# A mixture-of-experts block: normalised rows in the gather, scale and bias at its eviction

## The chip, the cores and the metric

The kernel runs on one core of a Trainium2 chip. The metric is the device time of one execution in microseconds (us). Three runs of the kernel before took 1916.12, 1918.36 and 1924.67 us; the median is 1918.36 us.

## The reference

All data are float32. `x` is (1, 256, 1024): 256 tokens of 1024 values. The kernel computes two blocks in one launch. The change lies in the first one, between its mixer and its experts:

```python
h = layer_norm(x, ln_in_g, ln_in_b)
m = gated_mixer(h, ...)                                   # attention branches, gates, w_out
h = layer_norm(DEEPNORM_ALPHA * h + m, ln1_g, ln1_b)      # "LN1": (x - mean) * rsqrt(var + eps) * g + b
f = moe_ffn(h, ...)
h = layer_norm(DEEPNORM_ALPHA * h + f, ln2_g, ln2_b)

def moe_ffn(t, ...):                                      # 32 experts, top 4
    logits = t @ w_router + b_router
    top_val, top_idx = top_k(logits, 4)
    gate = softmax(top_val)
    # for each expert e, on the rows of t routed to it:
    hb = rows @ w_exp_in[e] + b_exp_in[e]                 # 1024 x 2048
    g, u = min(hb[:, :1024], 7), clip(hb[:, 1024:], -7, 7)
    y = (g * sigmoid(1.702 * g) * (u + 1)) @ w_exp_out[e] + b_exp_out[e]
    # and the gate-weighted sum of a token's four rows
```

The second block (conditioned norms, a recurrent mixer, an attention and two MLPs) follows and is not touched.

## The kernel before

Tokens lie in two tiles of 128 (t = 0, 1). The mixer ends with the product with `w_out` and `join`, which leaves the sum in `x_tm`. Then comes what is here called the routing (L747 to L825). For each t VectorE takes mean and variance, GpSimd the power -0.5 (`rsqrt_g`, L189), VectorE normalises in place (L784). TensorE transposes the normalised rows (L790), VectorE and ScalarE evict them to `h1T`, and eight matmuls with the router's weights `wr` give the logits (L800). `wr` already has the norm's scale in it, and `brt` the router's bias with the norm's bias. VectorE finds the four largest (MAX8, FIND_INDEX8, L803 to L805) and builds the mask `M` of 128 tokens by 32 experts (L806, L808). Four small matmuls turn the masks into each token's rank within its expert (L818 to L821). Beside this chain `h1`, the rows that the experts read, gets the norm's scale and bias: the product for t = 0 on VectorE (L798), the one for t = 1 and both additions on GpSimd (L811, L813). `bcs` holds scale and bias spread over all partitions.

Each expert has 64 slots. `gather` builds the selection masks `sel` (VectorE, L886: slot number equal to rank) and multiplies `h1` by them on TensorE (L895), in two halves of four 128-column groups; each half is evicted by one ScalarE copy (L897) into `xg`, the experts' rows with the features on the partitions. From expert 2 on one gather serves two experts, which makes it 128 wide. The weights come as tiles of 2 MB, six per expert, through three rings of SBUF buffers (3, 4 and 1 tiles), all issued on SyncE's queue.

`step(e)` is written out for each expert: `up_tile` 0 (L922, names pg and pu); in odd steps the gather for the next two experts, first half; the transposes of the expert before (aT); `up_tile` 1; the transposed scatter mask (sT); `down_tile` (py, L953) of the expert before and its copy ys; `up_tile` 2; the gather's second half; `combine`; `up_tile` 3; the SwiGLU on VectorE and ScalarE. `combine` multiplies ys by sT into four banks pc (L966), and VectorE adds each to the accumulator `facc` (L971), which has the memory of `bcs`. Before each expert's tiles its bias is put into the two accumulating banks by matmuls with a column of the identity (L771); `first_bias` does this for experts 0 and 1 during the routing. `facc_init` after step 0 sets `facc` to ALPHA times `h1` (L995). PSUM has two tags ("b" and "g") of four banks each, handed out in turn; gathers, transposes, py and pc share "b".

What is wrapped in `keep` or `pin` stands on its engine (TensorE, SyncE's queue) in the order of the code. The other instructions are placed by a scheduler, and `issue_after(x)` keeps them behind x. Each engine runs its own queue in order and waits on semaphores. Between steps 20 and 21 a loop serves experts with more than 64 rows; on these inputs it has no turn, but the engines meet at its barrier.

Of the kernel before, what the change touches and what calls it, by code (L numbers as in the profile page):

```python
# [72 lines left out]
def tile_kernel(  # L73
# [668 lines left out]
    wo = [wcols(w_out[0], 0, 1024, k0=4 * i, kc=4, pool=ring, pin=True) for i in range(2)]  # L742
    spread(ln1_g, ln1_b)
    o = [banks("wo") for _ in range(2)]

# [28 lines left out]
    def first_bias(e, i):  # L774
        expert_bias(first_acc[e][i], ident[:, 4 * e:4 * e + 4], i, keep)

    pl = bank("lg")
    h1T = [tmp("h1T") for _ in range(4)]
    mv = small("ln1mv", 4).rearrange("p (t k) -> p t k", t=2)
    rs = small("ln1r", 2)  # L780
    for t in range(2):
        stats(x_tm[:, t], t, mv, "ln1")
        rsqrt_g(rs[:, t:t + 1], mv[:, t, 1:2], 1e-5)
        normed = V.tensor_scalar(x_tm[:, t], x_tm[:, t], mv[:, t, 0:1], rs[:, t:t + 1], op0=ALU.subtract, op1=ALU.mult).ins  # L784
    first_bias(0, 0)
    for t in range(2):
        for hf in range(2):
            p = bank("h1T")
            for c in range(4):
                keep(T.transpose(p[:, c * 128:(c + 1) * 128], x_tm[:, t, (4 * hf + c) * 128:(4 * hf + c + 1) * 128],  # L790
                                 ident))
            if hf:
                S.copy(h1T[2 * t + 1], p)
            else:
                V.tensor_copy(h1T[2 * t], p)
        if t == 0:
            with tc.issue_after(normed):
                V.tensor_tensor(h1[:, 0], x_tm[:, 0], bcs[:, 0], op=ALU.mult)  # L798
        for k in range(8):
            keep(T.matmul(pl[:, 32 * t:32 * t + 32], h1T[2 * t + k // 4][:, (k % 4) * 128:(k % 4 + 1) * 128], wr[:, k, :], start=k == 0,  # L800
                          stop=k == 7, skip_group_check=True))
        V.tensor_tensor(lg[:, t], pl[:, 32 * t:32 * t + 32], brt, op=ALU.add)
        V.max(m8[:, t], lg[:, t])  # L803
        V.max_index(i8[:, t], m8[:, t], lg[:, t])
        V.tensor_copy(f8[:, t], i8[:, t])  # L805
        V.tensor_scalar(Mr[:, t], slot_i[:, 0:32], f8[:, t, 0:1], None, op0=ALU.is_equal)  # L806
        for j in range(1, 4):
            V.scalar_tensor_tensor(Mr[:, t], slot_i[:, 0:32], f8[:, t, j:j + 1], M[:, t],  # L808
                                   op0=ALU.is_equal, op1=ALU.add)
    with tc.issue_after(mark["G"]):  # L810
        G.tensor_tensor(h1[:, 1], x_tm[:, 1], bcs[:, 0], op=ALU.mult)  # L811
        for t in (1, 0):
            G.tensor_tensor(h1[:, t], h1[:, t], bcs[:, 1], op=ALU.add)  # L813

    first_bias(0, 1)
    first_bias(1, 0)
    pr = bank("rank")
# [5 lines left out]
    V.tensor_scalar(rr, rr, -1.0, None, op0=ALU.add)  # L823
    first_bias(1, 1)
    V.tensor_copy(cnt, pr[:, 64:96])  # L825
# [54 lines left out]
    def gather(rank_aps, pin=lambda i: i):  # L880
# [9 lines left out]
        def half(hf):  # L890
            p = bank("xg")
            for kc in range(4):
                i, r = divmod(4 * hf + kc, 2)
                for t in range(2):
                    pin(T.matmul(p[:, kc * 128:kc * 128 + w], h1[:, t, 256 * i + r:256 * (i + 1):2], sel[:, t, 0:w],  # L895
                                 start=t == 0, stop=t == 1))
            S.copy(xg[:, 4 * hf:4 * hf + 4, 0:w], p.rearrange("p (k s) -> p k s", k=4)[:, :, 0:w])  # L897

# [92 lines left out]
    def facc_init():  # L991
        next(ada0, None)
        with tc.issue_after(first_sel):
            for t in range(2):
                V.tensor_scalar(facc[:, t], h1[:, t], ALPHA, None, op0=ALU.mult)  # L995

# [691 lines left out]
```

## Time and profile before

| | |
|---|---|
| runs, median | 1918.36 us (1916.12 to 1924.67) |
| the profiled execution | 1921.77 us |
| its span, first to last instruction | 1920.0 us |
| mean granted TensorE clock | 0.972 |
| TensorE busy | 1833.3 us, 95% |
| VectorE, ScalarE, GpSimd busy | 799.4, 557.3, 91.1 us |
| DMA | 595.84 MB, mean 310 GB/s |

The span is one execution recorded on the chip. The busy shares are averages over stages with different limits, so the views below are read by stage. PEclk is the granted TensorE clock as a share of full speed, 1.00 for the upper level and 0.50 for the lower; a value between them is a mean over a stretch. DMA share is the mean busy share of the core's 16 DMA engines.

### The profile page before, as it was taken

The numbers are of one execution on the slowest core, as the hardware profiler recorded it, in microseconds if no ns is written. First come the engines' busy times: TensorE is split into PE (matmuls) and PEld (weight loads), VectorE is DVE, ScalarE is ACT, GpSimd is POOL, SyncE is SP. The second block draws the span as 40 slices with busy tenths as digits, with TensorE's granted clock in tenths as the row PEclk, the third lists the DMA queues.
The fourth block names the chain that finished last, engine by engine and source line by source line (L and its number), as shares of the span: only waits on it lengthen the run. The fifth ranks groups of instructions, "written<-read, shape, count | busy, mean of one in ns | idle before, by whom it ended". The sixth has DMA issues, their size and how long they took to land.

```text
span 1920.0 us, 23489 instructions
## 1 busy us (share of the span) xinstructions
PE 1833.3 (95%) x9861; PEld 1106.0 (58%) x9861; DVE 799.4 (42%) x1388; ACT 557.3 (29%) x869; POOL 91.1 (5%) x106
## 2 busy tenths in 40 slices
PE   7999989999999999985999999899999999999999
PEld 6867743333333333322333333688888965778997
DVE  6756741121211221220221122667754465665555
ACT  4645301110011110000101110554544454564443
POOL 3000100000000000000000000200100011000000
PEclk9989979998999999997999999999999999999999
DMA  8667868998999999998999999774666565434452
GB/s 291 243 219 264 346 252 330 428 420 360 425 427 428 427 428 427 428 427 336 427 428 427 428 427 416 268 254 148 250 252 249 213 239 179 153 131 154 176 196 89
DMA packets 100302, 595.84 MB, mean 310 GB/s; under 512 B 7533, under 2 KB 8002, under 8 KB 75362
## 3 DMA queue, kind: packets, MB, share of 16 engines
q1 hardware_dynamic: 85874, 540.68, 69.9%
q0 software_dynamic: 14288, 53.63, 8.0%
q8 instruction: 78, 1.28, 0.3%
q14 instruction: 30, 0.25, 0.0%
q10 hardware_dynamic: 32, 0.01, 0.0%
HBM read 593.24 MB, written 1.06 MB: 310 GB/s over the span
## 4 chain that ended last, share of the span: by engine, by line
PE 80%; DMA 8%; issue 5%; DVE 4%; POOL 1%; ACT 1%; SPq 0%; POOLq 0%; DVEq 0%; ACTq 0%
PE pg L922 11%; PE py L953 11%; PE pu L922 11%; PE xg L895 4%; DMA w<-in_w_exp_in_dram 4%; DMA wa<-in_ada_w_dram 3%; PE hid L271 3%; PE hid L270 3%; PE hid L269 3%; PE pc L966 3%; PE acc L254 3%; PE acc L255 3%; PE acc L256 3%; PE adp L628 2%; PE pu L771 2%
## 5 line engine op out<-in xcount | busy, mean ns | idle before, releaser
L199 DVE TENSOR_TENSOR wl<-w,wh 128x1024 fp32r<-128x1024 f32 x244 | 301.2, 1235 | 231.5 <-ACT wh L198 230.9
L971 DVE TENSOR_TENSOR bcs<-bcs,pc 128x512 f32<-128x512 f32 x124 | 76.9, 682 | 661.5 <-PE pc L966 661.5
L198 ACT CAST wh<-w 128x1024 fp32r<-128x1024 f32 x244 | 255.9, 1049 | 315.3 <-PE acc L256 85.2
L922 PE MATMUL pg<-w,xg 128*64 128x512 f32 x1016 | 262.0, 605 | 1.2 <-DMA w<-in_w_exp_in_dram 1.2
L922 PE MATMUL pu<-w,xg 128*64 128x512 f32 x1016 | 257.1, 595 | 0.0
L953 PE MATMUL py<-w,aTs 128*64 128x512 f32 x1024 | 226.8, 595 | 0.0
L922 PEld LDWEIGHTS pu<-w,xg 128*64 128x64 f32 x1016 | 73.6, 138 | 147.1 <-issue 147.1
L922 PEld LDWEIGHTS pg<-w,xg 128*64 128x64 f32 x1016 | 67.8, 138 | 139.0 <-issue 131.6
L953 PEld LDWEIGHTS py<-w,aTs 128*64 128x64 f32 x1024 | 70.7, 137 | 133.2 <-issue 132.7
L270 PE MATMUL hid<-xhl,wh 128*128 128x256 f32 x512 | 145.4, 284 | 0.0
L271 PE MATMUL hid<-xhl,wl 128*128 128x256 f32 x512 | 145.3, 284 | 0.0
L269 PE MATMUL hid<-xhl,wh 128*128 128x256 f32 x512 | 145.2, 284 | 0.0
L270 PEld LDWEIGHTS hid<-xhl,wh 128*128 128x128 f32 x512 | 98.5, 192 | 2.2 <-issue 1.7
L269 PEld LDWEIGHTS hid<-xhl,wh 128*128 128x128 f32 x512 | 98.5, 192 | 2.1 <-ACT xhl L1255 1.7
L271 PEld LDWEIGHTS hid<-xhl,wl 128*128 128x128 f32 x512 | 98.5, 192 | 0.8 <-issue 0.8
L897 ACT COPY xg<-xg 128x512 f32<-128x512 f32 (+1 forms) x34 | 19.0, 560 | 265.8 <-PE xg L895 265.8
L254 PE MATMUL acc<-wh,hh 128*128 128x512 f32 x240 | 94.5, 394 | 0.0
L255 PE MATMUL acc<-wl,hh 128*128 128x512 f32 x240 | 93.7, 390 | 0.0
L256 PE MATMUL acc<-wh,hh 128*128 128x512 f32 x240 | 93.6, 390 | 0.0
L895 PEld LDWEIGHTS xg<-sel,h 128*128 128x128 f32 x544 | 71.3, 208 | 33.9 <-issue 33.5
L895 PE MATMUL xg<-sel,h 128*128 128x128 f32 (+1 forms) x544 | 77.7, 300 | 6.0 <-DVE sel L886 5.9
L958 ACT COPY ys<-py 128x512 f32<-128x512 f32 x32 | 18.7, 585 | 213.9 <-PE py L953 213.9
(529 smaller groups left out, 2666.7 us busy)
## 6 DMA issues: line engine op xcount, KB each, us to landing
w<-in_w_exp_in_dram SPq DMA_DIRECT2D x125, 2048.0 KB, 16.5
w<-in_w_exp_out_dram SPq DMA_DIRECT2D x63, 2048.0 KB, 13.4
w<-in_mlp_w_dram SPq DMA_DIRECT2D x32, 2048.0 KB, 7.5
wa<-in_ada_w_dram POOLq DMA_DIRECT2D x38, 1024.0 KB, 7.4
w<-in_w_in_dram SPq DMA_DIRECT2D x9, 2048.0 KB, 10.0
w<-in_w_in_ab_dram SPq DMA_DIRECT2D x7, 2048.0 KB, 13.8
w<-in_w_qkv_dram SPq DMA_DIRECT2D x6, 2048.0 KB, 7.8
wa<-in_ada_w_dram POOLq DMA_DIRECT2D x20, 512.0 KB, 4.8
```

The source lines that it names most:

```text
L198: mark["S"] = S.copy(hi, src).ins
L199: mark["V"] = V.tensor_tensor(lo, src, hi.bitcast(F32), op=ALU.subtract).ins
L254: T.matmul(outs[t], hs, wh[:, j, :], start=a, stop=False)
L255: T.matmul(outs[t], hs, wl[:, j, :], start=False, stop=False)
L256: T.matmul(outs[t], ls, wh[:, j, :], start=False, stop=z)
L269: T.matmul(o, hs, xh[:, k + j, :], start=a, stop=False, skip_group_check=True)
L270: T.matmul(o, hs, xl[:, k + j, :], start=False, stop=False, skip_group_check=True)
L271: last = T.matmul(o, ls, xh[:, k + j, :], start=False, stop=z and m % 2 == 1, skip_group_check=True)
L895: pin(T.matmul(p[:, kc * 128:kc * 128 + w], h1[:, t, 256 * i + r:256 * (i + 1):2], sel[:, t, 0:w], start=t == 0, stop=t == 1))
L922: last = pin(T.matmul(p[64 * hv:64 * hv + 64, :], xg[:, 2 * i + r, a * 64:(a + 1) * 64], w[:, r, b0 + hv * 512:b0 + (hv + 1) * 512], start ...
L953: pin(T.matmul(py[64 * j:64 * j + 64, :], aT[:, r * 128 + i * 64:r * 128 + (i + 1) * 64], w[:, r, j * 512:(j + 1) * 512], start=i == 0 and ...
L971: V.tensor_tensor(f, f, pc[j], op=ALU.add)
```

## The change

`h1` now takes the normalised rows and nothing else (L784 becomes L791): the multiplications and additions with the norm's scale and bias go, on VectorE and on GpSimd. The gather reads these rows, and its eviction applies scale and bias, which are per partition there: four pieces of 128 columns for each half, in turn on VectorE (tensor_scalar, L904 of the new kernel) and on ScalarE (activation, L902), with scale and bias from `gbP`, a new constant that two DMAs on GpSimd's queue load. `facc_init` does eight scalar_tensor_tensor instead of two tensor_scalar, since it has scale and bias to apply too. Three of the four first biases stand ahead of the transposes, the fourth behind the second half's logits. Two spare matmuls (`idle_turn`), whose bank nobody reads, are put behind the first half's logits and ahead of the rank.

```diff
@@ -741,6 +741,10 @@
     fm(lambda t, c: mg[:, t, c * 128:(c + 1) * 128], evac_plain, "mT")
     wo = [wcols(w_out[0], 0, 1024, k0=4 * i, kc=4, pool=ring, pin=True) for i in range(2)]
     spread(ln1_g, ln1_b)
+    gbP = const.tile([128, 2, 4, 2], F32, name="gbP")
+    for i, v in enumerate((ln1_g, ln1_b)):
+        nc.gpsimd.dma_start(gbP[:, i], bass.AP(tensor=v.tensor, offset=v.offset, ap=[[2, 128], [256, 4], [1, 2]]))
+    gbP = gbP.rearrange("p a i r -> p a (i r)")
     o = [banks("wo") for _ in range(2)]
 
     def join(n, t):
@@ -774,6 +778,9 @@
     def first_bias(e, i):
         expert_bias(first_acc[e][i], ident[:, 4 * e:4 * e + 4], i, keep)
 
+    def idle_turn():
+        keep(T.matmul(bank("idle"), ident, bi, start=True, stop=True))
+
     pl = bank("lg")
     h1T = [tmp("h1T") for _ in range(4)]
     mv = small("ln1mv", 4).rearrange("p (t k) -> p t k", t=2)
@@ -781,24 +788,24 @@
     for t in range(2):
         stats(x_tm[:, t], t, mv, "ln1")
         rsqrt_g(rs[:, t:t + 1], mv[:, t, 1:2], 1e-5)
-        normed = V.tensor_scalar(x_tm[:, t], x_tm[:, t], mv[:, t, 0:1], rs[:, t:t + 1], op0=ALU.subtract, op1=ALU.mult).ins
-    first_bias(0, 0)
+        V.tensor_scalar(h1[:, t], x_tm[:, t], mv[:, t, 0:1], rs[:, t:t + 1], op0=ALU.subtract, op1=ALU.mult)
+    for e, i in ((0, 0), (0, 1), (1, 0)):
+        first_bias(e, i)
     for t in range(2):
         for hf in range(2):
             p = bank("h1T")
             for c in range(4):
-                keep(T.transpose(p[:, c * 128:(c + 1) * 128], x_tm[:, t, (4 * hf + c) * 128:(4 * hf + c + 1) * 128],
+                keep(T.transpose(p[:, c * 128:(c + 1) * 128], h1[:, t, (4 * hf + c) * 128:(4 * hf + c + 1) * 128],
                                  ident))
             if hf:
                 S.copy(h1T[2 * t + 1], p)
             else:
                 V.tensor_copy(h1T[2 * t], p)
-        if t == 0:
-            with tc.issue_after(normed):
-                V.tensor_tensor(h1[:, 0], x_tm[:, 0], bcs[:, 0], op=ALU.mult)
         for k in range(8):
             keep(T.matmul(pl[:, 32 * t:32 * t + 32], h1T[2 * t + k // 4][:, (k % 4) * 128:(k % 4 + 1) * 128], wr[:, k, :], start=k == 0,
                           stop=k == 7, skip_group_check=True))
+        if t == 0:
+            idle_turn()
         V.tensor_tensor(lg[:, t], pl[:, 32 * t:32 * t + 32], brt, op=ALU.add)
         V.max(m8[:, t], lg[:, t])
         V.max_index(i8[:, t], m8[:, t], lg[:, t])
@@ -807,13 +814,8 @@
         for j in range(1, 4):
             V.scalar_tensor_tensor(Mr[:, t], slot_i[:, 0:32], f8[:, t, j:j + 1], M[:, t],
                                    op0=ALU.is_equal, op1=ALU.add)
-    with tc.issue_after(mark["G"]):
-        G.tensor_tensor(h1[:, 1], x_tm[:, 1], bcs[:, 0], op=ALU.mult)
-        for t in (1, 0):
-            G.tensor_tensor(h1[:, t], h1[:, t], bcs[:, 1], op=ALU.add)
-
-    first_bias(0, 1)
-    first_bias(1, 0)
+    first_bias(1, 1)
+    idle_turn()
     pr = bank("rank")
     keep(T.matmul(pr[:, 0:64], ur, Mr.rearrange("p t e -> p (t e)"), start=True, stop=False, skip_group_check=True))
     keep(T.matmul(pr[:, 32:64], onr, Mr[:, 0], start=False, stop=False, skip_group_check=True))
@@ -821,7 +823,6 @@
     keep(T.matmul(pr[:, 64:96], onr, Mr[:, 1], start=False, stop=True, skip_group_check=True))
     V.scalar_tensor_tensor(rr, pr[:, 0:64].rearrange("p (t e) -> p t e", t=2), 1.0, M, op0=ALU.add, op1=ALU.mult)
     V.tensor_scalar(rr, rr, -1.0, None, op0=ALU.add)
-    first_bias(1, 1)
     V.tensor_copy(cnt, pr[:, 64:96])
     st1.close()
 
@@ -894,7 +895,13 @@
                 for t in range(2):
                     pin(T.matmul(p[:, kc * 128:kc * 128 + w], h1[:, t, 256 * i + r:256 * (i + 1):2], sel[:, t, 0:w],
                                  start=t == 0, stop=t == 1))
-            S.copy(xg[:, 4 * hf:4 * hf + 4, 0:w], p.rearrange("p (k s) -> p k s", k=4)[:, :, 0:w])
+            for kc in range(4):
+                c = 4 * hf + kc
+                dst, src = xg[:, c, 0:w], p[:, kc * 128:kc * 128 + w]
+                if kc % 2:
+                    S.activation(dst, src, AF.Identity, bias=gbP[:, 1, c:c + 1], scale=gbP[:, 0, c:c + 1])
+                else:
+                    V.tensor_scalar(dst, src, gbP[:, 0, c:c + 1], gbP[:, 1, c:c + 1], op0=ALU.mult, op1=ALU.add)
 
         return xg, half
 
@@ -991,8 +998,14 @@
     def facc_init():
         next(ada0, None)
         with tc.issue_after(first_sel):
-            for t in range(2):
-                V.tensor_scalar(facc[:, t], h1[:, t], ALPHA, None, op0=ALU.mult)
+            g_, b_ = bcs[:, 0], bcs[:, 1]
+            h_ = [tmp("fh") for _ in range(2)]
+            for n in range(2):
+                cols = slice(512 * n, 512 * (n + 1))
+                V.scalar_tensor_tensor(h_[n], h1[:, 1, cols], ALPHA, g_[:, cols], op0=ALU.mult, op1=ALU.mult)
+                V.scalar_tensor_tensor(facc[:, 0, cols], h1[:, 0, cols], ALPHA, g_[:, cols], op0=ALU.mult, op1=ALU.mult)
+                V.scalar_tensor_tensor(facc[:, 0, cols], b_[:, cols], ALPHA, facc[:, 0, cols], op0=ALU.mult, op1=ALU.add)
+                V.scalar_tensor_tensor(facc[:, 1, cols], b_[:, cols], ALPHA, h_[n], op0=ALU.mult, op1=ALU.add)
 
     def ln2_rows():
         for i, v in enumerate((ln2_g, ln2_b)):
```

On TensorE, from the first bias to the last rank matmul, the order before is the following (pg and pu are the accumulators of experts 0 and 1, h1T the transposes, lg the logits):

```order
L771 MATMUL pg<-bi,ident 64x512 x2
L790 MATMUL h1T<-ident,x_tm 128x128 x8
L800 MATMUL lg<-wr,h1T 128x32 x8
L790 MATMUL h1T<-ident,x_tm 128x128 x8
L800 MATMUL lg<-wr,h1T 128x32 x8
L771 MATMUL pu<-bi,ident 64x512 x2
L771 MATMUL pg<-bi,ident 64x512 x2
L818 MATMUL rank<-M,uor 128x64
L819 MATMUL rank<-M,uor 128x32
L820 MATMUL rank<-M,uor 128x32
L821 MATMUL rank<-M,uor 128x32
L771 MATMUL pu<-bi,ident 64x512 x2
```

The same place of TensorE's queue in the changed kernel, up to the first rank matmul:

```order
L775 MATMUL pg<-bi,ident 64x512 x2
L775 MATMUL pu<-bi,ident 64x512 x2
L775 MATMUL pg<-bi,ident 64x512 x2
L798 MATMUL h1T<-ident,h_82 128x128 x8
L805 MATMUL lg<-wr,h1T 128x32 x8
L782 MATMUL idle<-bi,ident 128x512
L798 MATMUL h1T<-ident,h_82 128x128 x8
L805 MATMUL lg<-wr,h1T 128x32 x8
L775 MATMUL pu<-bi,ident 64x512 x2
L782 MATMUL idle<-bi,ident 128x512
L820 MATMUL rank<-M,uor 128x64
```

Two biases moved from behind the logits to ahead of the transposes, one from behind the rank to ahead of it, and a spare matmul stands behind the first logits and another ahead of the rank.

On VectorE, at the end of expert 0's SwiGLU (sg, uc) and ahead of the overflow loop's tables (ia, ib), the order before is:

```order
L935 TENSOR_TENSOR sg<-sg,gc 128x512 [waits Activation_49]
L589 TENSOR_TENSOR modT_476<-ada,abT 128x4 [waits PE_49]
L938 SCALAR_TENSOR_TENSOR uc<-uc,sg 128x512 [waits DVE_49]
L592 SCALAR_TENSOR_TENSOR scl_478<-modT_476,vT 128x8 [waits DVE_49]
L1042 TENSOR_TENSOR ia<-slot_i,pre 128x512
L1043 TENSOR_TENSOR ib<-slot_i,cum 128x512
```

The same place on VectorE in the changed kernel (bcs is the accumulator, h_82 the rows h1):

```order
L945 SCALAR_TENSOR_TENSOR uc<-uc,sg 128x512 [waits DVE_49]
L592 SCALAR_TENSOR_TENSOR scl_478<-modT_476,vT 128x8 [waits DVE_49]
L1005 SCALAR_TENSOR_TENSOR fh<-h_82,bcs 128x512 [waits DMAHW0_49]
L1005 SCALAR_TENSOR_TENSOR fh<-h_82,bcs 128x512
L1006 SCALAR_TENSOR_TENSOR bcs<-h_82,bcs 128x512 [waits DVE_49] x2
L1007 SCALAR_TENSOR_TENSOR bcs<-bcs 128x512 [waits DMAHW4_49,DVE_49]
L1007 SCALAR_TENSOR_TENSOR bcs<-bcs 128x512 [waits DVE_49]
L1008 SCALAR_TENSOR_TENSOR bcs<-bcs,fh 128x512 [waits DVE_49] x2
L1055 TENSOR_TENSOR ia<-slot_i,pre 128x512
```

The accumulator's start stood far ahead of this place, right behind the first selection masks; its eight instructions are now between the SwiGLU and the tables.

On TensorE, at the combine of a gather step (step 1; xg is the gather's second half), before:

```order
L895 MATMUL xg<-sel,h_82 128x128 x7
L966 MATMUL pc<-ys,sTs 128x512 [waits Activation_49]
L966 MATMUL pc<-ys,sTs 128x512 [waits PE_49] x2
L966 MATMUL pc<-ys,sTs 128x512 [waits Activation_49]
L922 MATMUL pg<-w,xg 64x512 [waits DMAHW1_49]
```

And after, at the same place:

```order
L896 MATMUL xg<-sel,h_82 128x128 x7
L973 MATMUL pc<-ys,sTs 128x512 [waits DVE_49,Activation_49]
L973 MATMUL pc<-ys,sTs 128x512 [waits PE_49] x2
L973 MATMUL pc<-ys,sTs 128x512 [waits DVE_49]
L929 MATMUL pg<-w,xg 64x512 [waits DMAHW1_49]
```

The instructions are the same; the fourth pc waited for ScalarE and now waits for VectorE. The instruction of VectorE that it waits for is the add (L978) of the first pc: in the gather steps the fourth pc is handed the bank of the first.

VectorE's queue at that place after (before, four adds stand there together):

```order
L904 TENSOR_SCALAR xg<-xg,gbP 128x128 [waits PE_49]
L978 TENSOR_TENSOR bcs<-bcs,pc 128x512 [waits PE_49]
L904 TENSOR_SCALAR xg<-xg,gbP 128x128 [waits Activation_49]
L978 TENSOR_TENSOR bcs<-bcs,pc 128x512 [waits PE_49] x3
```

Between the first add and the other three there is now a piece of the gather's eviction.

## Rows read from the trace of the kernel before

**Rows 1.** Windows by stage: start and end, length, busy time by engine (instructions), PEclk, DMA.

```profile
core 0: us, PE busy (x) PEld busy (x) DVE busy (x) ACT busy (x) POOL busy (x), PEclk, DMA share, GB/s
225.00:246.00 21.00, 18.10 (x80) 11.92 (x79) 16.99 (x45) 2.99 (x5) 9.10 (x6) 0.70 0.83 320
246.00:256.00 10.00, 10.00 (x40) 7.67 (x40) 4.88 (x29) 0.86 (x3) 0.00 (x0) 0.50 0.00 1
...
468.00:472.00 4.00, 4.00 (x19) 1.38 (x15) 0.00 (x0) 0.00 (x0) 0.00 (x0) 0.88 0.00 0
...
850.00:870.00 20.00, 5.66 (x26) 1.75 (x24) 5.58 (x10) 0.63 (x1) 0.00 (x0) 0.70 1.01 430
```

**Rows 2.** TensorE's waits from 245 to 1250: total us, times, longest.

```profile
PE pg L771 <- issue: 30.9, 1, 30.9
...
PE pg L922 <- DMA w<-in_w_exp_in_dram: 1.2, 1, 1.2
```

**Rows 3.** Chain of waits, 200 to 330: start us, us, engine and line.

```profile
236.94 2.40 DVE M L806
...
243.69 0.39 PE rank L818
244.70 1.91 PE pu L771 x4
246.60 7.02 PE xg L895 x32
...
259.08 2.03 PE xg L895 x16
...
262.12 0.86 PE pu L922 x4
...
276.39 0.60 DVE ia L1042
```

**Rows 4.** Timeline, 219 to 290: start, us, engine, line, operation, idle before.

```profile
230.39 1.07 PE L790 MATMUL h1T<-ident,x_tm 128*128 128x128 f32 x8 [1.72 <-DVE x_tm L784]
...
235.63 3.62 PE L800 MATMUL lg<-wr,h1T 128*128 128x32 f32 x16
...
236.96 4.64 POOL L813 TENSOR_TENSOR h<-h,bcs 128x1024 f32<-128x1024 f32 x2
...
241.57 0.18 DVE L803 MAX8 m<-lg 128x8 f32<-128x32 f32 x1
...
242.72 0.83 DVE L808 SCALAR_TENSOR_TENSOR M<-slot_i,f,M 128x32 fp32r<-128x32 f32 x3
...
246.33 1.29 DVE L995 TENSOR_SCALAR bcs<-h 128x1024 f32<-128x1024 f32 x2
...
275.62 0.69 DVE L938 SCALAR_TENSOR_TENSOR uc<-uc,sg 128x512 f32<-128x512 f32 x1
...
284.23 4.09 PE L895 MATMUL xg<-sel,h 128*128 128x128 f32 x16 [5.93 <-DVE sel L886]
```

**Rows 5.** Timeline of the combine in step 1.

```profile
305.21 1.99 PE L966 MATMUL pc<-ys,sTs 64*128 64x512 f32 x8
305.32 0.58 ACT L897 COPY xg<-xg 128x512 f32<-128x512 f32 x1 [4.88 <-PE xg L895]
306.37 2.48 DVE L971 TENSOR_TENSOR bcs<-bcs,pc 128x512 f32<-128x512 f32 x4 [21.35 <-PE pc L966]
307.13 1.94 PE L922 MATMUL pg<-w,xg 128*64 128x512 f32 x8
```

**Rows 6.** Chain of waits, 384 to 1240: the combines of steps 5 and 21.

```profile
423.67 1.92 PE pc L966 x8
...
913.78 1.92 PE pc L966 x8
```

**Rows 7.** Timeline of the kernel's start, 4 to 10.

```profile
7.35 0.80 DVE L345 TENSOR_SCALAR x_tm<-x_tm,ln0mv,ln0r 128x1024 f32<-128x1024 f32 x1
...
8.54 0.55 POOL L189 TENSOR_TENSOR ln0r<-rsq_v,mhalf 128x1 f32<-128x1 f32 x1 [1.55 <-DVE qsel L570]
```

**Rows 8.** Groups by line on GpSimd: busy us, mean ns of one, idle before.

```profile
L604 POOL DMA_DIRECT2D wa<-in_ada_w_dram x58 | 43.1, 744 | 423.8 <-PE adp L628 408.3 <-DMA wa<-in_ada_w_dram 13.0 <-issue 0.9
```

## Prediction

> **What bounds the kernel now.** I read the time first: the profiled execution took 1921.77 us around a span of 1920.0 us, 3.4 us above the median of the runs (1918.36 us). The sum below is made against the profiled execution and then carried down to the median.
>
> The second view is the table by stage [rows 1]. Before the first expert (225 to 246 us) TensorE is busy 18.1 of 21.0 us at a granted clock of 0.70, that is, part of it at the lower level (1.2 GHz, 0.5 of full speed) and part at the upper (2.4 GHz). From 246 to 256 us it is busy all the time at 0.50, and the weight stream stands still (0.00): the rings are full, and nothing is released before the first weight tile is used up. The reader is to see in the two later stretches who sets the end. From 468 to 472 us the stream stands still again while TensorE is fully busy: here the stream waits for TensorE. From 850 to 870 us it is the other way round: DMA share 1.01 at 430 GB/s, TensorE busy 5.66 of 20 us.
>
> The third view is TensorE's list of waits between 245 and 1250 us [rows 2]: one wait of 30.9 us at the barrier of the overflow loop (behind it the next row in length that weights cause is 1.2 us). So the expert stage has three parts. From the routing to about 471 us a delay of TensorE delays the stream, and with it the barrier. From 471 us to the barrier TensorE has about 31 us to spare, and a delay there costs nothing. After the barrier TensorE waits for no weights, and a delay counts in full again.
>
> The fourth view is the chain of waits through the routing [rows 3] beside the engines' timeline [rows 4].
>
> **The change part by part.** *Routing, taken out.* GpSimd adds rows for 4.64 us from 236.96 us on, and while it does so a mask operation of VectorE (L806) takes 2.40 us on the chain; three of the same size take 0.83 us together once GpSimd is done [rows 3, 4]. The MAX8 of the second half starts at 241.57 us though TensorE is through with its logits at 239.25 (235.63 + 3.62). From MAX8 to the rank matmul at 243.69 us it is 2.1 us. Without GpSimd the same steps can begin at 239.5, and rank stands at 241.6: 2.1 us earlier, with TensorE as slow as before.
>
> *Routing, put in.* Two more biases stand ahead of the transposes. A bias is 4 records; it takes 1.91 us at the lower level (L771), and the same shape takes 0.86 us at the upper (L922) [rows 3]. TensorE waits 1.72 us there for the normalised rows [rows 4], so at the upper level they fit, and at the lower they reach 2.1 us beyond it. Each spare matmul streams as many columns as a bias (512), so I bound it by one bias at either level, 0.86 to 1.91 us. The first lies ahead of the second half's transposes, the second in the wait for the masks.
>
> So both ends of this stage can be given. If TensorE works at the lower level all through, what GpSimd gave back (2.1) goes to the biases: gain 0. If it keeps the upper level all through, rank comes 2.9 us earlier; behind it the step from rank to the gather shrinks by 0.9 us, since the last bias has gone from there; the 32 gather records take twice 2.03 instead of 7.02 us (2.96 saved; L895 at 246.60 and at 259.08); and the first weight tile takes 3.43 (four times 0.86) instead of 5.46 us (2.03 saved: 253.62 to 259.08). That is 8.8 us. I take 4.0, near the middle, as the clock over the stage before was 0.70, between the levels, and filled waits move it up, but nothing in the rows says that it holds through rank and MAX8. **Term 1: -4.0 (0 to -8.8).**
>
> *The accumulator's start.* Two operations of 128x1024 (L995, 1.29 us together, at 246.33 us, where TensorE has the gather to do) become eight scalar_tensor_tensor of 128x512. In VectorE's order they now stand behind the first expert's SwiGLU and its modulation rows, ahead of the tables of the overflow loop, and these are ahead of the selection masks of the second gather. For exactly these TensorE waits: its gather at 284.23 us had been idle 5.93 us for a mask of VectorE [rows 4]. So nothing covers the eight. One of this kind and size takes 0.69 us (L938 at 275.62), and a step of such on the chain takes 0.60 us (L1042) [rows 3, 4]: 4.8 to 5.5 us; I take 5.0, as they follow one another. What is queued behind them on VectorE is the table, the masks and the sd of expert 1; only the selection masks are waited for. **Term 2: +5.0 (4.8 to 5.5).** If the part ahead of it is cut, TensorE comes to this wait earlier and so does VectorE; the term stays.
>
> *The gather's eviction.* One ScalarE copy of 128x512 (0.58 us) becomes four pieces, alternately VectorE and ScalarE, each waiting for the one ahead. A piece has a quarter of the copy's elements: it should take between a mask operation's 0.28 (0.83 / 3) and the whole copy's 0.58, so four take 1.1 to 2.3 us. The next half's 16 records take 2.03 us [rows 3], and the rows are wanted a step later, so the pieces themselves cost nothing; if they were wanted at once, it would be 0.5 to 1.7 us a step. What is not covered is a bank. Before, the fourth pc matmul of a gather step followed the copy at 305.32 us, done before the first pc was; the four pc run as two pairs, 1.99 us in all, and the next pg starts at 307.13 us [rows 5]. Now the two halves' banks are handed on in another order, and the fourth pc waits for VectorE's add of the first. That add starts at 306.37 us and takes, four in 2.48 us back to back, 0.69 us: it ends at 307.06, the fourth pc starts at 307.1 and takes 0.86 us by itself, and pg starts at 308.08 us: 0.95 us later. Bounds: 0, if the pair does not have to be split, and 1.3, if one of VectorE's pieces (0.28 us or a little more) comes ahead of the add. There is one such step for every second expert. Of steps 1, 3, 5 (the last at 423.67 us) and 21 to 29 (the first at 913.78 us) each counts [rows 6], those of 7 to 19 lie where TensorE has 31 us to spare. **Term 3: 8 x 0.95 = +7.6 (0 to 10.4).**
>
> *Scale and bias by partition.* Two DMAs are issued on GpSimd's queue at the very start, between its IOTA and the second norm's rsqrt, for which it waits 1.55 us anyway [rows 7]. Issues on this queue take 0.74 us [rows 8], so both take 1.49 us, and I take **term 4: +0.2 (0 to 0.3)**. That the transfer itself is late is excluded: its first use is 230 us later.
>
> Here a rule of the Trainium skill speaks against the change. SBUF — State Buffer, section "SBUF: two separate sides", says that while VectorE runs an operation that takes both port pairs, GpSimd can't write the descriptors of its DMAs. VectorE has an operation of 0.80 us at 7.35 us [rows 7], and if that is such a one, then by the rule the issues would wait for its end at 8.15, and the rsqrt would start at about 9.8 instead of 8.54: 1.2 us instead of 0.2, and the predicted time would be 1930.0. The rows show no issue beside such an operation, so the sum goes without it.
>
> **Sum.** -4.0 + 5.0 + 7.6 + 0.2 = +8.8 us: 1930.6 us against the profiled execution, 1927.2 against the median. I predict 1929.0, between the two, since the profiled execution lies within the runs' spread.
>
> **The rivals.** *TensorE keeps the upper level through the whole routing.* Term 1 is -8.8: +4.0, that is 1922.4 to 1925.8 us. For it: waits are filled by matmuls that need no data. Against: a stretch that is busy 18.1 of 21 us already shows 0.70.
>
> *TensorE stays at the lower level.* Term 1 is 0: +12.8, 1931.2 to 1934.6 us. For it: 246 to 256 us was busy without a break and was still at 0.50 [rows 1].
>
> *The fourth pc does not wait.* If the adds are early enough or the pair is not split, term 3 is 0: +1.2, 1919.6 to 1923.0 us. Against it: the add starts only when its pc is complete [rows 5].
>
> *The other side: the stream sets the end of the expert stage, from the first release on.* Then terms 2 and 3 lie under the weights, and only the earlier first release counts: -4.0 to -8.8, that is 1909.6 to 1917.8 us. It decides if the stream has no standstill after the first release. For it: 1.01 of the DMA engines at 430 GB/s for a long stretch. Against: the standstill at 468 to 472 us, and 1.2 us of waits for weights in a thousand [rows 1, 2].
>
> **How the numbers follow.** Forecast 0.57 (1924 to 1933 us by the bounds of the terms), upper level 0.13, lower level 0.14, free fourth pc 0.08, other side 0.08. A measurement can tell 0.5% from no change, 9.6 us: faster is below 1908.8 us, slower above 1927.95 us. Of the forecast 0.38 lies above that and 0.19 below; the lower level is slower, the upper level and the free pc are the same; of the other side 0.03 is faster, 0.05 the same. Slower 0.52, same 0.45, faster 0.03. The range runs from the middle of the free pc's case to the top of the lower level's: 1920 to 1935 us; outside are the other side, part of the free pc and the tails, together below 0.2.
>
> **What would show it.** In the profile after: MAX8 of the second half about 2 us after its logits at most, and mask operations of 0.25 us; the granted clock from 235 to 256 us tells the size of term 1, the first weight tile's end its sum (259.1 before; 255 by the forecast, 250 at the upper level, 259 at the lower). TensorE's wait for the selection mask is about 11 us instead of 5.9 (term 2). In gather steps the next pg starts 2.9 us after the first pc instead of 1.9, and TensorE's list of waits has a row of pc behind the add, of over 10 times 0.9 us (term 3). The barrier is later by the sum up to 471 us, about 4 us. I am wrong if the barrier comes earlier than before, if the wait for the mask has not grown, or if pg follows pc as closely as it did.

## The result and the profile after

The changed kernel takes 1930.91 us in the median of ten runs (1929.02 to 1933.83), the kernel before 1920.21 us in the median of nine runs beside it (a tenth took 3699.66 us and is left out). The ratio is 1.0051 (95% interval 1.0037 to 1.0066), so by it the change is 9.8 us (7.1 to 12.7) slower. Forecast were 1929.0 us and a range of 1920 to 1935. The profiled execution took 1933.71 us, span 1931.9 us, 11.9 us more than that of before.

Windows by stage of the kernel after (columns as in [rows 1]):

```profile
225.00:246.00 21.00, 19.06 (x110) 13.15 (x109) 14.57 (x52) 3.70 (x6) 1.25 (x3) 1.00 0.92 369
246.00:256.00 10.00, 10.00 (x44) 6.25 (x44) 3.90 (x25) 1.83 (x5) 0.00 (x0) 0.66 0.03 8
...
472.00:476.00 4.00, 4.00 (x22) 1.63 (x19) 0.00 (x0) 0.00 (x0) 0.00 (x0) 1.00 0.06 20
850.00:870.00 20.00, 15.39 (x72) 4.77 (x66) 5.58 (x10) 1.22 (x2) 0.00 (x0) 1.00 1.01 428
```

GpSimd is busy 1.25 instead of 9.10 us in the routing, and TensorE is at its upper level there all through; it falls to the lower one later, in the first gather. The standstill of the weight stream at about 470 us is still there, only 4 us later: TensorE still sets the time there.

TensorE's waits after, 245 to 1270 us [against rows 2, and 5.93 in rows 4]:

```profile
PE pg L775 <- issue: 25.4, 1, 25.4
PE xg L896 <- DVE sel L887: 10.7, 1, 10.7
```

The wait for the selection mask has grown by 4.8 us, and the wait at the barrier has shrunk by 5.5: TensorE comes there 9.7 us later, the barrier opens 4.3 us later.

The chain of waits after, 200 to 330 us [against rows 3]:

```profile
237.24 0.25 DVE M L813
...
242.65 0.27 PE rank L820
244.26 5.64 PE xg L896 x32
...
254.96 2.03 PE xg L896 x16
...
272.27 1.20 DVE fh L1005 x2
273.55 0.45 issue
274.00 0.69 DVE bcs L1006
274.68 1.20 DVE bcs L1007 x2
275.89 1.20 DVE bcs L1008 x2
277.09 0.60 DVE ia L1055
...
306.69 2.96 PE pc L973 x8
```

A mask operation takes 0.25 instead of 2.40 us. The first weight tile is used up at 254.96 instead of 259.08 us. The eight operations of the accumulator's start are on the chain, from 272.27 to 277.09, and pc has 2.96 us there. The timeline of that combine, step 1 [against rows 5]:

```profile
306.62 3.02 PE L973 MATMUL pc<-ys,sTs 64*128 64x512 f32 x8
306.72 0.41 DVE L904 TENSOR_SCALAR xg<-xg,gbP 128x128 f32<-128x128 f32 x1 [15.31 <-PE xg L896]
307.17 0.46 ACT L902 ACTIVATE xg<-xg,gbP 128x128 f32<-128x128 f32 x1 [5.37 <-DVE xg L904]
307.77 0.69 DVE L978 TENSOR_TENSOR bcs<-bcs,pc 128x512 f32<-128x512 f32 x1 [0.64 <-PE pc L973]
308.38 0.41 DVE L904 TENSOR_SCALAR xg<-xg,gbP 128x128 f32<-128x128 f32 x1
308.70 1.87 DVE L978 TENSOR_TENSOR bcs<-bcs,pc 128x512 f32<-128x512 f32 x3
...
309.57 1.94 PE L929 MATMUL pg<-w,xg 128*64 128x512 f32 x8
```

The wait itself stands with TensorE's weight loads (PEld in the views), which go ahead of the matmuls: the load for the fourth pc waits for the first add. From 245 to 1270 us there are 15 such waits, one in each gather step, and the kernel before has none:

```profile
308.52 0.29 PEld L973 LDWEIGHTS pc<-ys,sTs 64*128 64x128 f32 x2 [0.75 <-DVE bcs L978]
PEld pc L973 <- DVE bcs L978: 11.2, 15, 0.8
```

The first add ends at 308.46, and pg starts 1.1 us later, a pc by itself; from the first pc to pg it is 2.95 instead of 1.92 us. The chain after shows the 2.96 us in every gather step and 1.92 in the others; here steps 5 and 6, and 29 and 30 [against rows 6]:

```profile
428.12 2.95 PE pc L973 x8
454.89 1.92 PE pc L973 x8
...
1142.93 2.95 PE pc L973 x8
1169.71 1.92 PE pc L973 x8
```

The start of the kernel after [against rows 7 and 8]:

```profile
6.85 0.91 POOL L746 DMA_DIRECT2D gbP<-in_ln_g_dram  x1
...
7.34 0.90 DVE L345 TENSOR_SCALAR x_tm<-x_tm,ln0mv,ln0r 128x1024 f32<-128x1024 f32 x1
7.75 0.80 POOL L746 DMA_DIRECT2D gbP<-in_ln_b_dram  x1
...
8.65 0.57 POOL L189 TENSOR_TENSOR ln0r<-rsq_v,mhalf 128x1 f32<-128x1 f32 x1
```

The two issues took 1.71 us together, in part beside VectorE's operation, and the rsqrt is 0.11 us later; nearly all of that is VectorE's operation, which took 0.10 us longer.

Where the time went follows from the difference between the two traces at the same matmul, after less before:

| at | difference, us |
|---|---|
| end of the last product with w_out (ahead of the routing) | +2.5 |
| end of the first weight tile | -4.1 |
| first pc of step 1, step 3, step 5 | +1.4, +2.5, +4.5 |
| barrier opens; pc of step 21 | +4.3; +3.3 |
| pc of step 31 | +8.5 |
| first MLP of the second block (hid); end | +11.3; +11.9 |

Each gather step adds 1.04 us ahead of 428 us and behind the barrier; of the 2.0 us between steps 3 and 5 the other 1.0 was not traced. Two pieces were not foreseen: 2.5 us ahead of the routing and 2.8 us in the second block, whose code the change leaves as it was (gbP's two transfers aside).

### The profile page after: what moved, and what is told of

It reads as the page before. It is cut to its first block, busy times and chain, and to the rows that moved or that the text cites. A ratio compares the mean times of both kernels' runs of the same rounds, so it can differ in the third digit from the quotient of the medians.

```text
span 1931.9 us, 23634 instructions
## 1 busy us (share of the span) xinstructions
PE 1848.0 (96%) x9865; PEld 1106.4 (57%) x9865; DVE 822.5 (43%) x1461; ACT 568.5 (29%) x903; POOL 85.4 (4%) x105
## 4 chain that ended last, share of the span: by engine, by line
PE 82%; DMA 6%; issue 6%; DVE 4%; POOL 1%; ACT 1%; SPq 0%; POOLq 0%; DVEq 0%; ACTq 0%
PE pg L929 12%; PE py L960 12%; PE pu L929 11%; PE pc L973 4%; PE xg L896 4%; DMA wa<-in_ada_w_dram 3%; PE hid L271 3%; PE hid L270 3%; PE hid L269 3%; PE acc L254 3%; PE acc L255 3%; PE acc L256 3%; PE adp L628 2%; DMA w<-in_w_exp_in_dram 2%; PE pg L775 1%
## 5 line engine op out<-in xcount | busy, mean ns | idle before, releaser
L978 DVE TENSOR_TENSOR bcs<-bcs,pc 128x512 f32<-128x512 f32 x124 | 78.1, 682 | 316.7 <-PE pc L973 316.7
L904 DVE TENSOR_SCALAR xg<-xg,gbP 128x128 f32<-128x128 f32 (+1 forms) x68 | 27.3, 401 | 340.2 <-PE xg L896 322.6
L954 ACT COPY aTs<-aT 128x512 f32<-128x512 f32 x32 | 18.7, 585 | 274.8 <-PE aT L951 274.8
L896 PEld LDWEIGHTS xg<-sel,h 128*128 128x128 f32 x544 | 69.8, 204 | 38.2 <-issue 25.2
L896 PE MATMUL xg<-sel,h 128*128 128x128 f32 (+1 forms) x544 | 76.4, 296 | 11.8 <-DVE sel L887 11.7
## 6 DMA issues: line engine op xcount, KB each, us to landing
w<-in_w_in_dram SPq DMA_DIRECT2D x9, 2048.0 KB, 10.1
```

The source lines that it names most:

```text
L978: V.tensor_tensor(f, f, pc[j], op=ALU.add)
```

## The experiments

Each edit is against the changed kernel unless it says otherwise. Ratios are against the kernel before, with a 95% interval; the full change has 1.0051.

**routing_only**

```diff
-    gbP = const.tile(...)            # and its two DMAs
-            for kc in range(4): ...  # four pieces with scale and bias
+            S.copy(xg[:, 4 * hf:4 * hf + 4, 0:w], p.rearrange("p (k s) -> p k s", k=4)[:, :, 0:w])
-                V.scalar_tensor_tensor(...)      # the eight of facc_init
+            for t in range(2):
+                V.tensor_scalar(facc[:, t], h1[:, t], ALPHA, None, op0=ALU.mult)
```

> The changed kernel with the eviction of before (one ScalarE copy for each half), facc_init of before (two tensor_scalar) and without gbP: the norm's scale and bias are left out of the experts' rows and of the accumulator. So terms 2, 3 and 4 are gone and term 1 stands alone. Theory (term 1 -6.6 against the start of the routing, the later start of the routing in the profile after being a difference between executions): first weight tile used up 15.4 us after the routing's first normalisation starts less 6.6, that is about 23 us after it instead of 29.6; barrier some 5 to 7 us earlier than before; time 6 to 7 us under before, 1913 to 1917. Rival 1 (the 2.4 us by which the routing starts later come from the two gbP DMAs): the last product with w_out ends at 227.7 as before, and in the full change these DMAs cost 2.4 instead of 0.2. Rival 2 (the stream sets the end, so an earlier first release is all that counts): the same time, but the waits of TensorE for weights grow beyond 1.2 us.

Measured: 0.9975 (0.9960 to 0.9990), 4.8 us less than before, where 6 to 7 were expected; the first weight tile ends 24.9 us after the last product with w_out, the barrier opens 4.1 us earlier than in the first profile of before. pc takes 1.92 us and the wait for the mask is 5.9 us again. So the routing by itself is a gain, and all of the loss lies in what this run leaves out. The last product ends at 229.65 without gbP, which speaks against rival 1.

**facc_late**

```diff
-        if e == 0:
-            facc_init()
+                if e == 1:           # behind the gather of step 1, issue_after(mark["sel"])
+                    facc_init()
```

> The changed kernel with the eight scalar_tensor_tensor of the accumulator's start behind the second gather's selection masks instead of ahead of the overflow loop's tables. Theory: TensorE's wait for the selection mask falls from 10.7 to 5.9 us, pc of step 1 comes 4.8 us earlier, and the time is 4 to 5 us less than the full change (about 1926). Rival (the wait is set by something else, or the later accumulator delays the first combine): the wait stays at about 10.7, or pc's adds in step 1 come later than pc and the time does not change (1931).

Measured: 1.0043 (1.0026 to 1.0059). The wait is 5.8 us (`PE xg L896 <- DVE sel L887: 5.8, 1, 5.8`), and pc of step 1 comes 5.7 us earlier than in the full change (300.95 against 306.62). At the end of the expert stage 3.6 us are left of it and in the medians 2.8: the term is right at its place, and a part is given back later.

**copy_then**

```diff
+            S.copy(xg[:, 4 * hf:4 * hf + 4, 0:w], p.rearrange("p (k s) -> p k s", k=4)[:, :, 0:w])
             for kc in range(4):
-                (VectorE or ScalarE, from the bank)
+                V.tensor_scalar(dst, dst, gbP[:, 0, c:c + 1], gbP[:, 1, c:c + 1], op0=ALU.mult, op1=ALU.add)
```

> The changed kernel, but a half of the gather is evicted by one ScalarE copy as before, and scale and bias are applied behind it by four VectorE tensor_scalar from SBUF to SBUF. The fourth pc of a gather step then follows the copy again. Theory (term 3): pc takes 1.92 us in all gather steps instead of 2.96, TensorE's path loses 3 x 1.04 up to 471 us and 5 x 1.04 behind the barrier, together about 8 us: 1922 to 1924. Rival (the wait of the fourth pc is covered elsewhere): pc takes 1.92 us and the time stays within 2 us of the full change.

Measured: 0.9999 (0.9987 to 1.0012), 1920.1 us. pc takes 1.92 us in every step (`914.26 1.92 PE pc L971 x8` in step 21), and from step 21 to step 31 the difference to the first profile of before stays within 0.1 us, where the full change loses 5.2. This one edit takes back the whole loss.

**before_again** and **before_third** are the kernel before, for more profiles of it.

> The kernel before once more, for a second profile of it. Theory (the 2.4 us ahead of the routing and the some 3 us in the second block by which the profile after is longer than that of before are differences between executions): the last product with w_out ends anywhere from 227 to 231 us, and the way from the first nT to the end differs from the first profile's by over 1 us. Rival (both belong to the change): 227.7 and 707.6 us as in the first profile, within 0.5 us.

> The kernel before a third time. From the end of the last product with w_out to the end of the first weight tile it took 31.4 us in the first profile (TensorE at its lower level to 257 us), and 25.1 us in the second and in scale_load_only, whose routing is the same (upper level from 244 us on). Theory (the lower level through the first gather is one of two ways in which executions of this routing go, and the prediction was worked out from the less common one): rank 16.0 us after the last product, the first weight tile's end at 25.1 us. Rival (both are about as common): 31 us.

Measured: the times of both theories came. In both new profiles the last product with w_out ends at 228.4 and the rank stands 16.03 us after it as in the first, but the first weight tile ends at 25.12 us after it instead of 31.35. The windows of before_third:

```profile
225.00:246.00 21.00, 18.21 (x84) 12.10 (x82) 17.00 (x44) 2.99 (x5) 9.10 (x6) 0.76 0.88 343
246.00:256.00 10.00, 9.98 (x68) 7.06 (x68) 5.22 (x32) 1.25 (x4) 0.00 (x0) 1.00 0.19 39
```

Against [rows 1] it is the second window: 1.00 instead of 0.50. Three of four profiles with this routing (scale_load_only below is the fourth) are of this kind; that the first kind is the less common one is not shown, since these three executions took 1914.4 to 1919.9 us, all below the median of before's runs (1920.7 to 1921.8). Against the two new profiles the full change is 5.7 us later at step 1, 9.4 at the barrier and 14.2 at step 31, so the table above holds against the first profile alone. Nor does the profile of routing_only show a gain against before_again (pc of step 1 at 300.94 and 300.96 us); its gain stands in the times. The spans are 1918.1 and 1912.7 us with the same expert stage; before_again loses the 5 us in the second block, so that block differs between executions by as much as what the table above left open.

**scale_load_late** and **scale_load_only**: gbP's two DMAs moved behind the second half's rsqrt, and gbP and its DMAs alone, put into the kernel before.

```diff
+        G.tensor_copy(gbv[:, i, 0, 0:1], rs[:, 1:2])        # scale_load_late: makes the DMA wait
+        nc.gpsimd.dma_start(gbv[:, i], ...)
```

> The changed kernel with the two gbP DMAs issued on GpSimd's queue behind the second half's rsqrt (a one-column copy into gbP ahead of each makes them wait) instead of at the start. In the three profiles of kernels with gbP at the start the DMA engines move 310 to 330 GB/s at 10.5 to 13.5 us where the others move 385 to 400, the first weights land 0.8 us later, and the last product with w_out ends 2.5 to 2.9 us later than in the first profile of before. Theory (term 4 is about +1.5 instead of +0.2, by the many short pieces of these transfers beside the first weights and not by the issue): 380 to 400 GB/s there, the last product ends at 228 to 229.3 us, and the time is 1 to 2 us less than the full change. Rival (executions differ by that much anyway, as routing_only without gbP shows with 229.65): it ends at 229.5 to 230.5 and the time is the same within 1 us.

> The kernel before, and in addition gbP and its two DMAs at the start; nobody reads it. In all five profiles of kernels with gbP one power operation of GpSimd in the second block (L1243 there) takes 1.47 us, in the four without it 0.55 us, and TensorE waits 0.9 us longer there. Theory (term 4 belongs to gbP's being there, not to the eviction): 0.9 us longer at this place, 320 GB/s instead of 390 at 10.5 to 13.5 us, time 0.5 to 2 us over before. Rival (the 0.9 us comes from the rest of the change): 0.55 us there, and the time is before's within 0.5 us.

Measured: 1.0052 (1.0032 to 1.0072) and 0.9995 (0.9982 to 1.0009). My theory fell in both. The DMA engines do move 388 instead of 315 GB/s at 10.5 to 13.5 us once gbP is late, but the last product ends at 231.7 us, later than in any other profile, and gbP alone costs before nothing that can be measured. GpSimd's power operation in the second block takes 0.55 us in scale_load_only, so gbP is not what makes it 1.47 us (more on it under what stays open).

**no_spare** and **gpsimd_only**: routing_only without the spare matmuls, and in addition with the first biases where they stood before.

```diff
-        if t == 0:                    # no_spare
-            idle_turn()
-    idle_turn()
-    for e, i in ((0, 0), (0, 1), (1, 0)):    # gpsimd_only as well: the order of before
-        first_bias(e, i)
+    first_bias(0, 0)
```

> As routing_only (scale and bias of the norm left out), without the two spare matmuls. From the end of the last product with w_out to the rank it was 16.0 us in both profiles of before and 12.5 in the full change, and to the end of the first weight tile 31.4 and 25.1 us in before and 24.8 us in four kernels with the new routing. Theory (the spare matmuls only move where TensorE falls to its lower level): rank 0.5 us earlier or later (12.0 to 13.0), the end of the first weight tile between 23 and 27 us, time the same as routing_only within 2 us. Rival (they hold the upper level through the logits): granted clock of 0.5 to 0.7 from 232 to 244 us instead of 1.00, rank 14 us or more after the last product.

> As no_spare, and the biases stand where they stood before: of the routing's changes only GpSimd's leaving is left (scale and bias of the norm left out). Theory (GpSimd's part by itself is 2.1 us): rank 13.9 us after the last product with w_out instead of 16.0, mask operations of 0.25 us, and the granted clock as in before (0.5 to 0.7 from 232 to 244 us); the end of the first weight tile 23 us after it if TensorE is at its upper level by then, as in the second profile of before, and 29 us if not; time 2 us under before. Rival (GpSimd's leaving is all of the gain): rank 12.5 us after it, as in the full change.

Measured: 0.9984 (0.9969 to 0.9999) and 0.9966 (0.9952 to 0.9979). The table has, from the end of the last product with w_out, the rank and the end of the first weight tile, and the mean granted clock in windows of 4 us from the span's start (the last product ends between 227.7 and 230.2 in these):

| kernel | rank | first tile | 236-240 | 240-244 | 244-248 | 248-252 | 252-256 |
|---|---|---|---|---|---|---|---|
| before (first profile) | 16.0 | 31.4 | 0.50 | 0.50 | 0.50 | 0.50 | 0.50 |
| before_again, before_third, scale_load_only | 16.0 | 25.1 | 0.50 | 0.50 | 0.96 to 0.99 | 1.00 | 1.00 |
| full change | 12.5 | 24.8 | 1.00 | 1.00 | 0.75 | 0.50 | 0.89 |
| no_spare | 12.4 | 27.3 | 0.60 | 0.50 | 0.50 | 0.50 | 0.76 |
| gpsimd_only | 13.2 | 22.3 | 1.00 | 0.57 | 1.00 | 1.00 | 1.00 |

In gpsimd_only the rank comes 2.9 us earlier than in before. That is not GpSimd's leaving alone: VectorE's product of 1.22 us (L798) went with it, and against what I expected TensorE is at its upper level from 236 to 240 us there, and the second half's logits take 1.97 us instead of 3.62. No run separates these. The biases, moved, bring 0.7 more at the rank (in gpsimd_only the masks are done at 242.08 us, but two biases at the lower level hold TensorE until 243.39), the spare matmuls nothing (12.4 without, 12.5 with). No kernel kept the upper level throughout: with the filled waits the lower level comes later, in the first gather. By these traces the first tile ends later with them: 24.8 to 24.9 us after the last product in all seven profiles with filled waits, 22.3 in gpsimd_only and in mended_old_order, which has the same order. The times of the three routings can't be told apart by their intervals, but filling the waits shows no gain over taking GpSimd off alone.

**three_mended** and **mended_old_order**: facc_late and copy_then together, the loop's tables built after step 8; the first with gbP late, the second with gpsimd_only's order.

```diff
-            later_consts()                     # after step 0
+            {2: load_bo, 4: ln2_rows, 6: out_bias, 8: later_consts}[e]()
```

> The changed kernel with the accumulator's start behind the second gather's masks, the copy of before ahead of the scaling (fourth pc free), gbP loaded late, and in addition the overflow loop's tables (later_consts) built after step 8 instead of step 0, so that nothing stands ahead of the second gather's masks on VectorE. Theory (the costs found add up, and TensorE sets the end up to 471 us): no wait for masks at 279 to 285 us (before 5.9, full change 10.7), pc 1.92 us, and 1931 - 10.7 - 8.0 - 1.5 = 1909 to 1912 us, 8 to 11 under before. Rival (once TensorE is 10 us earlier there, the weight stream sets the end of this part): waits of TensorE for weights of over 3 us ahead of the barrier and no standstill of the stream at about 460 us; 1914 to 1917 us.

> As three_mended (accumulator's start and the loop's tables late, fourth pc free), but gbP loaded at the start, the first biases where they stood before, and no spare matmuls: of the routing's changes only GpSimd's leaving. Theory (biases and spare matmuls bring nothing: gpsimd_only was at 0.9966 of before, no_spare at 0.9984, routing_only at 0.9975): rank 13.2 us after the last product with w_out, time the same as three_mended within 3 us, 1908 to 1913. Rival (they bring the 0.6 us of rank, 13.15 against 12.53, or hold the clock through the first gather): 3 us or more over three_mended.

Measured: 0.9953 (0.9933 to 0.9973), 1910.92 us, and 0.9957 (0.9938 to 0.9975), 1913.30 us. Both beat the kernel before and the full change; the costs add up as the stages say. TensorE has no wait for a mask at the second gather; one of 4.8 us now stands at 516 us in three_mended, behind the stream's standstill, and TensorE still waits 28 to 29 us at the barrier. pc of step 1 comes 14.4 to 14.8 us earlier than in the first profile of before, the barrier 11.1 to 11.7, the end of the expert stage 11.1 to 12.6; against before_again it is 10.1 to 10.5, 6.0 to 6.6 and 5.4 to 7.0.

**pieces_on_vector**

```diff
-                if kc % 2: S.activation(...)
+                V.tensor_scalar(xg[:, c, 0:w], p[:, kc * 128:kc * 128 + w], gbP[:, 0, c:c + 1], gbP[:, 1, c:c + 1], ...)
```

> The changed kernel with all four pieces of a gather half's eviction on VectorE (none on ScalarE). The fourth pc of a gather step then has the bank of the gather's second half again and waits for the last of its four pieces, which stand ahead of the four adds. Theory (the cost of term 3 is the time until the instruction that frees the fourth pc's bank, plus 0.86 us of a pc by itself): the pieces start 0.1 us after the first pc and are done some 1.2 to 1.5 us after it (0.41 us for one, less when they follow one another), so the four pc take 2.1 to 2.5 us instead of 2.96 and 1.92, and the time is 3 to 7 us less than the full change. Rival (the cost comes from the alternation of the two engines, not from the bank): 1.92 us as in copy_then, or 2.96 as in the full change.

Measured: 1.0027 (1.0013 to 1.0040). Timeline of step 1's combine in this kernel:

```profile
307.28 2.65 PE L970 MATMUL pc<-ys,sTs 64*128 64x512 f32 x8
307.39 1.37 DVE L900 TENSOR_SCALAR xg<-xg,gbP 128x128 f32<-128x128 f32 x4 [16.51 <-PE xg L896]
308.67 2.47 DVE L975 TENSOR_TENSOR bcs<-bcs,pc 128x512 f32<-128x512 f32 x4
309.86 1.94 PE L926 MATMUL pg<-w,xg 128*64 128x512 f32 x8
```

The last piece ends at 308.76, and pg starts 1.10 us later, as it does behind the add in the full change. The wait of the weight loads is now for the pieces (`PEld pc L970 <- DVE xg L900: 5.7, 15, 0.4`). So the price is set by the instruction that frees the fourth pc's bank; 2.58 us lies between the 1.92 and the 2.96 of the others, a little above what I expected.

## Why the prediction was right

*Term 2, the accumulator's start: right.* Forecast +5.0; the wait grew from 5.9 to 10.7 us, +4.8, and went back to 5.8 in facc_late, with pc of step 1 5.7 us earlier.

*Term 3, the fourth pc: right, the largest term.* Forecast 0.95 us in each of eight steps; it is 1.04, since pg starts 1.1 us after the first add's end, not 1.0. (The working had a slip: 307.1 and 0.86 make 307.96 and not 308.08, which would be 0.83 us; so that the sum came close is in part chance.) copy_then, which only frees that bank early, takes the time from 1.0051 to 0.9999, and pieces_on_vector puts the price between. That steps 7 to 19 cost nothing shows at the barrier: TensorE reaches the barrier 9.7 us later, but it opens only 4.3 us later. The sign that was named for it came, in the list of the weight loads: 15 waits of pc behind the add, of 0.75 us each. The list of the matmuls alone has no such row; there the wait lies within a group of eight records and shows as 2.96 us of busy time.

*Term 1, the routing: the size by time about right, the reasoning mixed.* Forecast -4.0; routing_only is 4.8 us (1.9 to 7.7) under before. GpSimd's part was taken as 2.1 us to the rank; gpsimd_only has 2.9, but with the logits 1.65 us shorter by the clock, so its own part stays open. For the upper level 2.9 us to the rank was put down without a working; the full change, at that level until there, has 3.5. And I took the clock of one profile as that of the kernel: in three further profiles with this routing TensorE was back at its upper level in the window from 244 to 248 us, the first tile ended 25.1 us after the last product, and against these the full change gains 0.3 us there, not 6.6. Neither end that I bounded came: the full change has the upper level to 244 us and the lower behind it. That 1929.0 us lies within 2 us of the result is therefore partly luck: the sum was made against the one profile in which term 1 can be seen, and 2.5 and 2.8 us elsewhere were not in it.

*Term 4, scale and bias: right that it is small.* The rsqrt is 0.11 us later, and scale_load_only costs nothing measurable. The rule of the Trainium skill (SBUF — State Buffer, "SBUF: two separate sides"), by which the issues would wait for VectorE's operation, is not what this row shows: an issue begun at 7.75 us took 0.80 us, near the mean of 0.74 [rows 8], though VectorE's operation went on to 8.24; the operation itself took 0.90 instead of 0.80. Whether that operation is of the kind that the rule means, no run here tells.

*The rivals.* The free fourth pc and the stream as the bound are refuted by copy_then and by the standstill at 472 to 476 us. The two rivals on the clock were both too simple, as the table shows.

*What stays open.* Where parts of the gains are given back between step 1 and the end (facc_late: 5.7 us at step 1, 3.6 at step 31) was not traced step by step. And a power operation of GpSimd in the second block takes 1.47 us instead of 0.55, with TensorE waiting 0.9 us longer, in all seven kernels that have the scaled eviction and the new facc_init, and in none of the seven profiles without. The traces show what it waits for. In the full change VectorE's tensor_tensor of 128x1024 (L1251) starts ahead of it, and it ends 0.41 us behind that operation; in before it starts 0.02 us ahead of the same operation (L1238) and takes its 0.55:

```profile
1367.12 1.22 DVE L1251 TENSOR_TENSOR wl<-w,wh 128x1024 fp32r<-128x1024 f32 x1
1367.28 1.47 POOL L1243 TENSOR_TENSOR nrs<-nv,mhalf 128x1 f32<-128x1 f32 x1 [0.16 <-DVE nv L1242]
1358.52 0.55 POOL L1230 TENSOR_TENSOR nrs<-nv,mhalf 128x1 f32<-128x1 f32 x1 [0.16 <-DVE nv L1229]
1358.54 1.25 DVE L1238 TENSOR_TENSOR wl<-w,wh 128x1024 fp32r<-128x1024 f32 x1
```

All fourteen profiles follow this. Why VectorE's operation starts 0.18 us earlier in the seven is not settled.

## What to carry to other kernels

When an eviction is cut into pieces, look up which bank the next accumulators get and which instruction frees it: 1.04 us in a step, unseen in the list of the matmuls' waits and plain in that of the weight loads, cost more than the whole routing gained. Work that is moved off one engine comes to rest somewhere on another's queue; look for the next thing there that somebody waits for. One profile's clock is one execution's: bound what hangs on it by both levels and by a second profile.

## What the runs showed of the hardware

While GpSimd worked through rows of 128x1024, small operations of VectorE were held until it was done: the cast at L805 ended at 236.90 us (GpSimd's product at 236.88), the two mask operations begun at 236.94 and 239.40 at 239.34 and 241.65 (its additions at 239.30 and 241.60), and they took 2.40 and 2.25 instead of 0.24 us [rows 3, 4]. A copy from PSUM (235 us) and a MAX8 beside the product took what they take without it, 0.69 and 0.18 us. The other way round, GpSimd's power operation was held by VectorE's tensor_tensor, 1.47 instead of 0.55 us. TensorE's fall to its lower level came 5.4 to 5.8 us after the last product with w_out in the four profiles with the routing of before and 15.9 to 17.0 us after it with the filled waits, but it did not go. Two transfers in runs of 8 bytes (gbP) lowered the DMA engines from 389 to 315 GB/s at 10.5 to 13.5 us, at no measurable cost.
